# Where side work stands: sums of down weights moved by a few heads, and norm rows turned before they leave the chip

## The chip, the cores and the metric

The kernel runs on one core of one Trainium2 chip. The metric is the device time of one execution in microseconds (us). The core has TensorE (PE, with its weight loads as PEld), VectorE (DVE), ScalarE (ACT), GpSimd (POOL) and SyncE (SP), which here issues most DMAs; each engine works off its own queue in order, and waits on semaphores.

## What is computed

One layer of a diffusion backbone over 2048 latent tokens of width 1024, with 256 context tokens. Cut to what matters here:

```python
h   = modulate(rms_norm(x, g1), shift_a, scale_a)     # adaLN: modulation from c
q, k, v, g, f = split(h @ w_in)                        # 4 retention heads of 128, a Fourier part of 512
r   = retention(q, k, v)  (two scans, chunks of 128, states started from the context) * silu(g)
z   = real(fft2(f over positions and channels))        # 4 groups
m   = concat(r, z) @ w_out                             # output projection
x   = x + gate_a * rms_norm(m, g2)
h   = modulate(rms_norm(x, g3), shift_b, scale_b)
y   = conv3 over each image row of (h @ w_up); y = gate * value
x   = x + gate_b * rms_norm(y @ w_down, g4)
```

The inputs are fp32. The output has the shape of x.

## The kernel before

**Arithmetic.** A product of two fp32 matrices is made of three passes: each operand is split into a rounded part and the rest (`split`: ACT casts `hi`, VectorE subtracts to get `lo`), and `mm3` (lines 90, 91, 92) multiplies hi·hi, hi·lo and lo·hi into one PSUM tile. Tokens lie in the free dimension in four blocks `b` of 512, channels in the partitions in eight tiles of 128.

**Stages, in order of time.** Modulation, context and the weights of its keys `wk` (to 80 us); four blocks of v products with their norm, `adaw` being the modulation weights for the second half of the layer (80 to 186); heads 0 to 3, about 100 us each, as generators of strips (`k_strip`, `q_strip`: products of one block) and cores (`k_core`, `q_core`: states and chunk products), walked by one loop over `units`; the Fourier stage (to about 750); the output projection, 32 steps of `mix_mm(b, n)` (block b, output tile n), into `psmix` tiles that ACT seeds with the Fourier half (`seed_mix`, two steps ahead); then two passes of up products and two of down products.

**Who sets the order.** The code is written in one order, and a scheduler reorders it on each engine: an instruction whose inputs and buffers are there may move ahead of others. `tc.keep_in_program_order(i)` ties an instruction to its written place. Within the output projection a table `steps` says after which of the 32 steps a thing is written (`at(t, f, ...)`).

**Down sums.** The up and down products of later stages use sums of weight blocks. `w_sums()` makes those of the down weights in 22 chunks: two loads of 256 KB (line 205), four VectorE operations of 128×256 (line 220), one store of 512 KB to `wd` (line 222). Its buffer pool holds two chunks. It is written in the Fourier stage (`some_sums`, one `next` per operation).

**Norm rows.** A norm over channels needs sums over partitions: `sum_cols` multiplies squares with ones into `pc` (line 160), VectorE scales (`rp`, line 128), POOL raises to the power −0.5 (line 129) and leaves a column tile of 128×4 (`rcm` for the projection, `r2c` for the second norm, `rcf` at the end). To multiply along tokens it must become a row on all partitions: for the first blocks by TensorE and ACT (`bcast_row`: `pb`, `rr_`), for others through DRAM: `row_out` writes the column (line 133), `row_in` reads it back to all partitions (line 138).

**Hand-over.** In the last steps of the output projection the first up products start (`psu`); their weights come by `ur<-in_w_up` (line 1152), are split to `u_a`, and are taken by `operands`. `mt` and `m` (lines 964, 967), `h`, `b`, `t` (1037, 1040, 1041) are what is made of the projection's result: residual, norm, modulation and the sums of blocks. `late_h` makes `xn` of a block that is needed only later.

## Time and profile before

| | us |
|---|---|
| median of 3 runs | 2201.43 |
| the 3 runs | 2195.55, 2201.43, 2203.13 |
| the profiled execution | 2195.93 |
| its span in the trace | 2194.2 |
| PE busy in the span | 2076.4 (95%) |
| DVE busy | 1615.2 (74%) |
| ACT busy | 1009.2 (46%) |
| POOL busy | 616.7 (28%) |

The span is that of the instructions on the core; 1.7 us of the execution lie around it. Busy time is counted over the whole span, and the stages differ. The granted clock of TensorE is written as a share of its full speed, 2.4 GHz; where it is 0.5 the other level, 1.2 GHz, was granted.

### The profile page before, as it was taken

The numbers are of one execution on the slowest core, as the hardware profiler recorded it, in microseconds if no ns is written. First come the engines' busy times: TensorE is split into PE (matmuls) and PEld (weight loads), VectorE is DVE, ScalarE is ACT, GpSimd is POOL, SyncE is SP. The second block draws the span as 40 slices with busy tenths as digits, with TensorE's granted clock in tenths as the row PEclk, the third lists the DMA queues.
The fourth block names the chain that finished last, engine by engine and source line by source line (L and its number), as shares of the span: only waits on it lengthen the run. The fifth ranks groups of instructions, "written<-read, shape, count | busy, mean of one in ns | idle before, by whom it ended". The sixth has DMA issues, their size and how long they took to land.

```text
span 2194.2 us, 28116 instructions
## 1 busy us (share of the span) xinstructions
PE 2076.4 (95%) x9819; PEld 1711.4 (78%) x9819; DVE 1615.2 (74%) x2346; ACT 1009.2 (46%) x1754; POOL 616.7 (28%) x496
## 2 busy tenths in 40 slices
PE   7899899999899977989989999999999999999996
PEld 3777778888798866778778888887887888878886
DVE  6876877767566387998898886778777777775557
ACT  4342233324444566544545554545555455553441
POOL 4101122323101243242343342021333334331025
PEclk9999999999999988999999999999999999999998
DMA  8676643232562155664564478665355655386653
GB/s 306 213 242 216 192 139 92 100 96 95 146 223 100 52 199 139 183 207 176 183 205 159 154 275 297 218 242 177 135 187 197 185 185 178 135 272 224 200 154 130
DMA packets 202590, 395.20 MB, mean 180 GB/s; under 512 B 31816, under 2 KB 69584, under 8 KB 202448
## 3 DMA queue, kind: packets, MB, share of 16 engines
q1 hardware_dynamic: 194416, 367.07, 51.6%
q0 software_dynamic: 7600, 26.23, 3.3%
q8 instruction: 77, 1.26, 0.2%
q14 instruction: 65, 0.53, 0.1%
q10 hardware_dynamic: 432, 0.11, 0.0%
HBM read 275.33 MB, written 118.00 MB: 179 GB/s over the span
## 4 chain that ended last, share of the span: by engine, by line
PE 56%; DVE 22%; DMA 10%; issue 6%; ACT 3%; POOL 2%; SPq 1%; DVEq 0%; ACTq 0%; POOLq 0%
PE psu L90 8%; PE psu L91 8%; PE psu L92 8%; PE psd L90 5%; PE psd L91 5%; PE psd L92 5%; DMA ur<-in_w_up 2%; DVE u_a L83 2%; DVE y L1259 1%; DVE u_s L83 1%; DVE fd L638 1%; DMA wsum<-in_w_down 1%; DMA adaw<-in_wadaB 1%; PE pada L86 1%; DMA wd<-wsum 1%
## 5 line engine op out<-in xcount | busy, mean ns | idle before, releaser
L83 DVE TENSOR_TENSOR dlo<-draw,dhi 128x1024 fp32r<-128x1024 f32 x154 | 200.3, 1323 | 113.7 <-ACT dhi L82 102.4
L91 PE MATMUL psd<-dlo,dhi 128*128 128x512 f32 (+1 forms) x660 | 247.1, 375 | 2.9 <-DVE dlo L83 2.9
L92 PE MATMUL psd<-dhi,dlo 128*128 128x512 f32 (+1 forms) x660 | 246.2, 375 | 0.0
L1297 POOL TENSOR_TENSOR y<-y,y 128x512 f32<-128x512 f32 x82 | 127.0, 1549 | 388.5 <-DVE y L1260 274.5
L82 ACT CAST dhi<-draw 128x1024 fp32r<-128x1024 f32 x154 | 159.7, 1051 | 162.2 <-PE psd L92 116.5
L90 PE MATMUL psd<-dhi 128*128 128x512 f32 (+1 forms) x660 | 209.4, 375 | 0.6 <-DVE cx L1558 0.6
L91 PE MATMUL psu<-t,u_s 128*128 128x512 f32 x492 | 194.1, 395 | 1.4 <-DVE t L83 1.4
L90 PE MATMUL psu<-t,u_s 128*128 128x512 f32 x492 | 194.9, 396 | 0.0
L92 PE MATMUL psu<-t,u_s 128*128 128x512 f32 x492 | 193.9, 394 | 0.0
L83 DVE TENSOR_TENSOR u_a<-ur,u_a 128x512 fp32r<-128x512 f32 x147 | 139.7, 953 | 61.3 <-ACT u_a L82 60.8
L90 PE MATMUL psu<-b,u_a 128*128 128x512 f32 x424 | 165.6, 391 | 3.1 <-ACT u_a L82 1.9
L91 PE MATMUL psu<-b,u_a 128*128 128x512 f32 x424 | 165.2, 390 | 0.0
L92 PE MATMUL psu<-b,u_a 128*128 128x512 f32 x424 | 165.2, 390 | 0.0
L91 PEld LDWEIGHTS psd<-dlo,dhi 128*128 128x128 f32 x660 | 124.2, 188 | 25.6 <-DVE dlo L83 3.3
L92 PEld LDWEIGHTS psd<-dhi,dlo 128*128 128x128 f32 x660 | 124.2, 188 | 22.3
L90 PEld LDWEIGHTS psd<-dhi 128*128 128x128 f32 x660 | 123.3, 188 | 23.2 <-DVE cx L1558 0.8
L82 ACT CAST u_a<-ur 128x512 fp32r<-128x512 f32 x147 | 90.6, 620 | 103.0 <-PE psu L92 92.3
L1256 ACT ACTIVATE y<-psu,cb,cw 128x512 f32<-128x512 f32 x135 | 104.2, 775 | 19.0 <-DVE psu L1405 13.7
L83 DVE TENSOR_TENSOR u_s<-us,u_s 128x512 fp32r<-128x512 f32 x103 | 84.7, 823 | 38.4 <-ACT u_s L82 38.3
L91 PEld LDWEIGHTS psu<-t,u_s 128*128 128x128 f32 x492 | 94.1, 191 | 22.0 <-DVE t L83 1.9
L90 PEld LDWEIGHTS psu<-t,u_s 128*128 128x128 f32 x492 | 94.1, 191 | 19.9 <-ACT psu L1394 0.9
L92 PEld LDWEIGHTS psu<-t,u_s 128*128 128x128 f32 x492 | 93.8, 191 | 20.0
(438 smaller groups left out, 5313.9 us busy)
## 6 DMA issues: line engine op xcount, KB each, us to landing
ur<-in_w_up SPq DMA_DIRECT2D x74, 512.0 KB, 5.5
draw<-wd SPq DMA_DIRECT2D x88, 256.0 KB, 5.6
draw<-ft SPq DMA_DIRECT2D x88, 256.0 KB, 5.8
ft<-y SPq DMA_DIRECT2D x36, 512.0 KB, 5.5
draw<-in_w_down SPq DMA_DIRECT2D x66, 256.0 KB, 5.1
draw<-fb SPq DMA_DIRECT2D x66, 256.0 KB, 5.3
xt<-in_xT SPq DMA_DIRECT2D x56, 256.0 KB, 4.0
adaw<-in_wadaB SPq DMA_DIRECT2D x24, 512.0 KB, 6.5
```

The lines of the kernel that those rows point to most:

```text
L82: nc.scalar.copy(hi, src)
L83: nc.vector.tensor_tensor(lo, src, hi.bitcast(F32), op=ALU.subtract)
L86: nc.tensor.matmul(ps, l, r, start=start, stop=stop)
L90: nc.tensor.matmul(ps, lhi, rhi, start=start, stop=False, skip_group_check=on)
L91: nc.tensor.matmul(ps, lhi, rlo, start=False, stop=False, skip_group_check=on)
L92: nc.tensor.matmul(ps, llo, rhi, start=False, stop=stop, skip_group_check=on)
L638: tc.keep_in_program_order(nc.vector.tensor_tensor(o_, a_, b_, op=op))
L1256: nc.scalar.activation(y, ps, AF.Identity, bias=cb[:, j:j + 1], scale=cw[:, j, 1:2])
L1259: nc.vector.scalar_tensor_tensor(y3[:, :, 1:64], p3[:, :, 0:63], cw[:, j, 0:1], y3[:, :, 1:64], ALU.mult, ALU.add)
L1297: nc.gpsimd.tensor_tensor(y1, y1, y2, op=ALU.mult)
```

## The change

Five edits. (1) All eight `wk` tiles are cast by ACT; POOL and VectorE only subtract. (2) The down sums are written in heads 1 to 3, one step after every fourth piece, and in smaller doses in the Fourier stage; the first load of each chunk is tied to its place. (3) `row_out` turns the column by a TensorE product with the identity into PSUM (`prow`, 4×128), VectorE copies it (`rowt`), and the DMA writes four runs of 128 numbers. `row_in` is tied to its place. (4) The writing of rows is taken out of `mix_cols` and `x2_cols` into functions of its own, called a step later. (5) In the output projection, the loads of `rt`, the first norms, the first load of up weights and the first four splits stand at other steps, and those four casts are tied.

```diff
-        def split(hi, lo, src):
-            nc.scalar.copy(hi, src)
+        def split(hi, lo, src, tie=False):
+            c = nc.scalar.copy(hi, src)
+            if tie:
+                tc.keep_in_program_order(c)
             nc.vector.tensor_tensor(lo, src, hi.bitcast(F32), op=ALU.subtract)
...
         def row_out(rc, n, name, eng=None):
             d = dp.tile([n * P], F32, tag="row_" + name, name="row_" + name)
-            (eng or nc.sync).dma_start(d.rearrange("(i p) -> p i", p=P), rc)
+            pr = pmt([n, P], "prow")
+            mm(pr, rc, ident, True, True)
+            t = cp.tile([n, P], F32, tag="rowt", name="rowt")
+            nc.vector.tensor_copy(t, pr)
+            (eng or nc.sync).dma_start(d.rearrange("(i p) -> i p", p=P), t)
             return d
...
         def row_in(rt, d, n, name, eng=None):
             rr = rt([P, n * P], "rr_" + name)
-            (eng or nc.sync).dma_start(rr, bass.AP(tensor=d.tensor, offset=d.offset, ap=[[0, P], [1, n * P]]))
+            r = (eng or nc.sync).dma_start(rr, bass.AP(tensor=d.tensor, offset=d.offset, ap=[[0, P], [1, n * P]]))
+            tc.keep_in_program_order(r)
...
-                        nc.sync.dma_start(w[:, 2 * i:2 * i + 2], A["w_down"][k + KH * i].rearrange("p (n c) -> p n c", n=2)[:, :, c])
+                        ld = nc.sync.dma_start(w[:, 2 * i:2 * i + 2], A["w_down"][k + KH * i].rearrange("p (n c) -> p n c", n=2)[:, :, c])
+                        if i == 0:
+                            tc.keep_in_program_order(ld)
...
-            if kt % 2:
-                nc.scalar.copy(w[:, 0], src)
-                nc.gpsimd.tensor_tensor(w[:, 1], src, w[:, 0].bitcast(F32), op=ALU.subtract)
-            else:
-                nc.vector.tensor_copy(w[:, 0], src)
-                nc.vector.tensor_tensor(w[:, 1], src, w[:, 0].bitcast(F32), op=ALU.subtract)
+            nc.scalar.copy(w[:, 0], src)
+            (nc.gpsimd if kt % 2 else nc.vector).tensor_tensor(w[:, 1], src, w[:, 0].bitcast(F32), op=ALU.subtract)
...
                 npiece += 1
                 if npiece % (KSTEP if sf is k_strip else QSTEP) == 0:
                     next(folds, None)
+                if o.h and npiece % 4 == 2:
+                    some_sums(1)
...
                 p1 = zprod(2 * part, lt)
-                some_sums(2)
+                some_sums(1)
...
         def mix_cols(b):
             rcm[b] = cst([P, 4], f"rcm{b}", po_)
             sum_cols(accm[b], rcm[b], 4, po_)
-            if b > 1:
-                rowm[b] = row_out(rcm[b], 4, f"m{b}")
+
+        def mix_out(b):
+            rowm[b] = row_out(rcm[b], 4, f"m{b}")
...
         def x2_cols(b):
             sum_cols(accx[b], r2c[:, 4 * b:4 * b + 4], 4, po_)
-            if b:
-                r2d[b] = row_out(r2c[:, 4 * b:4 * b + 4], 4, f"n{b}")
+
+        def x2_out(b):
+            r2d[b] = row_out(r2c[:, 4 * b:4 * b + 4], 4, f"n{b}")
...
-                split(w[:, 0], w[:, 1], a[nme])
+                split(w[:, 0], w[:, 1], a[nme], not bb and len(early) < 4)
...
-                at(RS[0] * b + RS[1] * k // 2, load_r, b + 1, k)
+                at(KT * b + 1 + k, load_r, b + 1, k)
...
-            at(t + 6, x2_cols, b)
-            at(t + 7, x2_rows, b)
+            at(t + 7, x2_cols, b)
+            at(t + 8, x2_rows, b)
+        at(26, x2_out, 1)
         at(27, mix_cols, 2)
+        at(28, mix_out, 2)
...
-        at(26, lambda: up0.append(up_load(0)))
+        at(25, lambda: up0.append(up_load(0)))
         early = []
-        for n in range(4):
-            at(28, lambda: early.append(next(up0[0][2])))
...
+            if t in (28, 29):
+                early.extend(next(up0[0][2]) for _ in range(2))
...
         def rest_of_mix():
             mix_cols(3)
+            yield
+            mix_out(3)
+            yield
...
                 x2_cols(b)
+                yield
+                x2_out(b)
                 yield
```

Here RS was (8, 4) and KT is 8: the loads of the next block stood at steps 0, 2, 4 and 6 of a block, and stand at 1, 2, 3 and 4.

Where instructions come to stand, at three places. First VectorE at the beginning of head 1, before: the rotation of keys (`kT`), a difference of the Fourier part (`fd`), a scaled key (`kzb`) and the states `S`.

```order
L638 TENSOR_TENSOR fd_3_2462<-h_0_779 128x512
L561 TENSOR_SCALAR kzb<-ptk,EXT 128x512
L500 TENSOR_TENSOR kT_0_2350<-psk,rpt 128x512
L501 TENSOR_TENSOR kT_0_2350<-kT_0_2350,rpt 128x512
L502 TENSOR_TENSOR kT_0_2350<-kT_0_2350,sw 128x512
L575 SCALAR_TENSOR_TENSOR S_0_2467<-S_0_2467,EXT,pkv 128x128 x3
L575 SCALAR_TENSOR_TENSOR S_1_2471<-S_0_2467,EXT,pkv 128x128
```

The same place after:

```order
L643 TENSOR_TENSOR fd_3_2470<-h_0_779 128x512
L229 TENSOR_TENSOR wsum<-wsum 128x256 x3
L566 TENSOR_SCALAR kzb<-ptk,EXT 128x512
L229 TENSOR_TENSOR wsum<-wsum 128x256
L505 TENSOR_TENSOR kT_0_2350<-psk,rpt 128x512
L229 TENSOR_TENSOR wsum<-wsum 128x256
L506 TENSOR_TENSOR kT_0_2350<-kT_0_2350,rpt 128x512
L229 TENSOR_TENSOR wsum<-wsum 128x256
L507 TENSOR_TENSOR kT_0_2350<-kT_0_2350,sw 128x512
L580 SCALAR_TENSOR_TENSOR S_0_2476<-S_0_2476,EXT,pkv 128x128
```

Six sums stand between those operations. Before, the 88 stood in VectorE's order from the WK matrices to the end of head 0; now 13 stand at the end of head 0, 55 in head 1 and 20 in the key strips of head 2, none elsewhere.

Second, ACT at the end of the output projection, before: `m` leaves `psmix`, `psmix<-m` is a seed, `sq` a square for a norm, `u_a` the first splits of up weights.

```order
L1007 COPY m_3_5902<-psmix 128x512
L154 ACTIVATE sq<-psmix 128x512
L82 CAST u_a_7299<-ur_7219 128x512
L82 CAST u_a_7302<-ur_7219 128x512
L82 CAST u_a_7305<-ur_7220 128x512
L82 CAST u_a_7308<-ur_7220 128x512
L1041 ACTIVATE h_7311<-h_7311,modB 128x512
L82 CAST t_0_7318<-m_0_5899 128x512
L996 COPY psmix<-m_3_6094 128x512
L1007 COPY m_3_5966<-psmix 128x512
L1007 COPY m_3_6030<-psmix 128x512
```

The same place after:

```order
L1015 COPY m_3_5975<-psmix 128x512
L161 ACTIVATE sq<-psmix 128x512
L81 CAST t_0_7310<-m_0_5972 128x512
L1004 COPY psmix<-m_3_6149 128x512
L1015 COPY m_3_6032<-psmix 128x512
L1051 ACTIVATE h_7303<-h_7303,modB 128x512
L1015 COPY m_3_6092<-psmix 128x512
L1051 ACTIVATE h_7304<-h_7304,modB 128x512
L81 CAST b_1_7315<-h_7304 128x512
L81 CAST u_a_7322<-ur_7198 128x512
L81 CAST u_a_7325<-ur_7198 128x512
```

The last seed (`psmix<-m`) stood behind four `u_a` casts, and stands ahead of the first.

Third, SP's queue at that time, before: `row_n` and `row_m` are the rows, `x` stores of the projection's result, `xt` loads of the input.

```order
L133 DMA row_n_7144<-r2c 128x4x1
L1152 DMA ur_7219<-in_w_up 128x1024
L1009 DMA x_2_3_119<-m_3_6030 128x512
L1152 DMA ur_7220<-in_w_up 128x1024
L133 DMA row_m_7263<-rcm_7254 128x4x1
L1009 DMA x_3_3_123<-m_3_6094 128x512
L957 DMA xt_7798<-in_xT 128x512
L138 DMA rr_n_10637<-row_n_7144 128x512
L1152 DMA ur_7295<-in_w_up 128x1024
```

The same place after:

```order
L1162 DMA ur_7198<-in_w_up 128x1024
L1162 DMA ur_7199<-in_w_up 128x1024
L1017 DMA x_2_3_119<-m_3_6092 128x512
L139 DMA row_n_7221<-rowt 4x128
L1017 DMA x_3_3_123<-m_3_6149 128x512
L1017 DMA x_4_3_127<-m_3_5975 128x512
L139 DMA row_m_7297<-rowt 4x128
L1017 DMA x_5_3_131<-m_3_6032 128x512
```

The first two `ur` loads stand ahead of `row_n`, and both rows leave from `rowt`, a tile of 4×128.

## Rows read from the trace of the kernel before

**Rows 1.** Busy time of each engine by stretch of the span, core 0, with the mean granted TensorE clock (1.00 is full) and the DMA engines' busy share behind it: WK and context (39 to 80), v products (80 to 186), heads 0 to 3, output projection with the hand-over, the stage behind it, and the first down pass. Columns: stretch in us: its length, busy time (instructions) of PE, PEld, DVE, ACT, POOL, then PEclk, DMA share, GB/s.
```profile
39.00:80.00 41.00, 33.08 (x144) 26.25 (x145) 31.85 (x57) 18.68 (x39) 11.20 (x9) 0.86 0.48 160
80.00:186.00 106.00, 100.44 (x440) 81.20 (x440) 83.39 (x147) 45.23 (x74) 4.19 (x3) 0.95 0.73 233
186.00:292.00 106.00, 93.97 (x487) 78.28 (x485) 82.51 (x169) 28.61 (x79) 23.78 (x21) 0.95 0.65 206
292.00:387.00 95.00, 92.32 (x521) 78.64 (x520) 68.85 (x127) 31.20 (x89) 25.82 (x23) 1.00 0.35 99
387.00:486.00 99.00, 94.00 (x527) 79.78 (x526) 71.93 (x129) 31.36 (x89) 26.16 (x23) 1.00 0.32 95
486.00:586.00 100.00, 95.66 (x526) 80.83 (x524) 64.48 (x97) 42.64 (x94) 27.59 (x22) 0.98 0.43 121
...
752.00:861.00 109.00, 86.97 (x377) 70.04 (x376) 75.13 (x99) 69.06 (x128) 42.36 (x26) 0.87 0.57 158
861.00:1000.00 139.00, 130.30 (x558) 105.39 (x557) 130.31 (x179) 74.36 (x125) 50.83 (x29) 0.98 0.59 192
...
1300.00:1500.00 200.00, 200.00 (x884) 165.62 (x883) 145.14 (x152) 99.39 (x115) 46.52 (x52) 1.00 0.69 239
```

**Rows 2.** The tile `wsum` (the down sums): operation, count, duration in ns as min/median/max, first and last start in us; and, from the waits of SP's queue within 186 to 292 us, what SP stood on before a load of it (us in total, times, longest).
```profile
L220 DVE TENSOR_TENSOR wsum<-wsum x88: 408/418/1441, 62.6 to 297.4; 128x256 f32<-128x256 f32 x88
L205 SPq DMA_DIRECT2D wsum<-in_w_down x44: 539/600/1520, 36.3 to 281.3; - x44
...
SPq L205 <- DMA wd<-wsum: 25.2, 9, 5.9
```

**Rows 3.** TensorE's timeline at 55 to 60 us (start, length, engine, line and operation, and in brackets the idle time before it with what ended it), and the tile `wk`: two of its operations, and one line of who waited for it.
```profile
56.10 0.73 PE L90 MATMUL psc<-wk,hc 128*128 128x512 f32 x2 [3.00 <-DVE wk L414]
59.18 0.80 PE L91 MATMUL psc<-wk,hc 128*128 128x512 f32 x1 [2.35 <-DVE wk L415]
...
L411 ACT CAST wk<-wkr x4: 618/620/622, 53.6 to 55.2; 128x512 fp32r<-128x512 f32 x4
L412 POOL TENSOR_TENSOR wk<-wkr,wk x4: 1437/1450/1720, 54.3 to 58.5; 128x512 fp32r<-128x512 f32 x4
...
  ACT kz L424: 11.7, 1
```

**Rows 4.** v products: TensorE's timeline at two of its sums of squares, and VectorE's group of `wsum` within 80 to 186 us (busy us, mean ns, idle time before it and what ended that).
```profile
123.97 1.02 PE L160 MATMUL pc<-ones,acc 128*128 128x1 f32 x8 [1.92 <-DVE acc L155]
...
152.03 0.69 PE L160 MATMUL pc<-ones,acc 128*128 128x1 f32 x5 [2.31 <-DVE acc L155]
...
L220 DVE TENSOR_TENSOR wsum<-wsum 128x256 f32<-128x256 f32 x31 | 12.3, 419 | 6.9 <-DMA wsum<-in_w_down 6.7
```

**Rows 5.** Head 0 (186 to 292 us): one stall in TensorE's timeline, VectorE's group of `wsum`, and a small load's median landing time (issues, KB each, us); last, from SP's waits in head 1 (292 to 387), what the loads of v stood on.
```profile
266.28 0.66 PE L627 MATMUL pto<-ident,sT 128*128 128x128 f32 x2 [3.24 <-DVE sT L623]
...
L220 DVE TENSOR_TENSOR wsum<-wsum 128x256 f32<-128x256 f32 x45 | 20.5, 457 | 12.4 <-DMA wsum<-in_w_down 11.0 <-issue 0.8
...
S<-sini SPq DMA_DIRECT2D x2, 64.0 KB, 3.4
...
SPq L506 <- PE pkv L86: 15.5, 4, 6.9
```

**Rows 6.** Output projection: the stalls in TensorE's timeline, and two pieces of the chain of waits (start, length, what) at the sum of squares that `row_n` carries.
```profile
781.87 1.41 PE L160 MATMUL pc<-ones,accx 128*128 128x1 f32 x6 [4.06 <-DVE accx L155]
...
813.00 0.73 PE L90 MATMUL psmix<-rt,wr 128*128 128x512 f32 x2 [3.18 <-ACT rt L82]
816.45 0.80 PE L91 MATMUL psmix<-rt,wr 128*128 128x512 f32 x1 [2.72 <-DVE rt L83]
...
851.17 0.80 PE L90 MATMUL psmix<-rt,wr 128*128 128x512 f32 x1 [8.80 <-ACT psmix L996]
...
824.30 0.80 PE pc L160 x8
825.44 1.03 POOL r2c L129
```

**Rows 7.** The hand-over: ACT's timeline; the traffic of 826 to 852 us in 40 slices of 0.65 us; two DMA issues within it (count, KB each, median us to landing), and the first of them over the whole span; last, the window behind the hand-over with the columns of rows 1.
```profile
848.36 1.14 ACT L82 CAST u_a<-ur 128x512 fp32r<-128x512 f32 x2 [6.75 <-DMA ur<-in_w_up]
...
850.53 0.58 ACT L996 COPY psmix<-m 128x512 f32<-128x512 f32 x1
...
GB/s 0 0 3 0 0 13 13 25 69 25 38 44 38 25 25 13 25 19 63 309 236 391 373 376 320 167 63 16 60 35 22 38 69 91 227 221 224 293 356 384
...
ur<-in_w_up SPq DMA_DIRECT2D x4, 512.0 KB, 14.1
...
row_n<-r2c SPq DMA_DIRECT2D x1, 2.0 KB, 11.4
...
ur<-in_w_up SPq DMA_DIRECT2D x74, 512.0 KB, 5.5
...
852.00:866.00 14.00, 14.00 (x54) 11.34 (x54) 12.93 (x18) 10.62 (x20) 4.82 (x3) 0.85 0.67 252
```

**Rows 8.** First up pass: two stalls in TensorE's timeline; and, from the tile `row_n`, who waited for it (us, times).
```profile
942.93 0.50 PE L90 MATMUL psu<-t,u_a 128*128 128x512 f32 x1 [2.43 <-DVE psf L1408]
...
1153.21 0.79 PE L90 MATMUL psu<-t,u_a 128*128 128x512 f32 x1 [5.21 <-DVE psf L1408]
...
  POOL rr_n L138: 19.0, 2
```

15 lines of the change are left out of this document (7 added, 8 removed).

## Prediction

> **What bounds the kernel now.** I read the windows by stage first [rows 1]. TensorE is busy in nearly all of every stage, so what matters is where it isn't. A stage without loss exists: from 1300 to 1500 it is busy 200.00 of 200 us at granted clock 1.00. For the others I take as loss the idle time plus (1 − clock) times the stretch, since a stretch at half clock does half its work. That gives 7.9 + 5.7 = 13.7 us in 39–80 (the WK matrices), 5.6 + 5.3 = 10.9 in 80–186 (v products), 12.0 + 5.3 = 17.3 in head 0 (186–292), only 2.7, 5.0 and 6.3 in heads 1, 2 and 3, then 22.0 + 14.2 = 36.2 in the output projection with its hand-over to the up products (752–861), and 8.7 + 2.8 = 11.5 in 861–1000. What is worth having lies in five places, and all five are touched by the diff.
>
> Next I asked what these stages hold that the quiet ones don't. The tile view of the sums [rows 2] shows 88 VectorE operations of 418 ns in the median and 44 loads, started from 36 to 297 us: although the code asks for them in the Fourier stage, 31 of them run in 80–186 (12.3 us) [rows 4] and 45 in head 0 (20.5 us) [rows 5]. The queue view shows SP standing 25.2 us in head 0 on `wd<-wsum`, a store's landing, before it may issue the next load [rows 2]; vb, fscr and strip loads stand in line behind that. The idle times of TensorE [rows 3 to 6] then name what comes last: VectorE nearly everywhere up to head 0, and at 851.17 a wait of 8.80 us for the ACT copy that seeds `psmix`, more than any other of these rows.
>
> **The change part by part.**
>
> *WK casts.* TensorE waits 3.00 and 2.35 us for a VectorE cast and subtraction of `wk` at 56–59 us, and the clock dip around it is in the 5.7 us of clock loss of that stretch [rows 1, 3]. VectorE casts four pages and subtracts four; after, ACT casts all eight at 0.62 us, 5.0 us in a row from about 53.6, and VectorE only subtracts. The first page is then ready near 54.2, and its product no longer waits until 56.10. The extra 2.5 us on ACT are covered: ACT waits 11.7 us behind its four casts [rows 3]. But POOL's four subtractions of 1.45 us end about where they did (54.8 + 5.8 = 60.6, before 58.5 + 1.7), so the last pages gain nothing. I take −4; bounds −1 (only the first page matters) and −8 (both waits and half the dip).
>
> *v products without sums.* 31 sums and some eight chunks of loads and stores leave. VectorE loses 12.3 us of work and a 6.7 us wait for a sum's load that blocked everything behind it [rows 4]. The stalls there that name VectorE sum to 1.92 + 2.31 = 4.2 us, each followed by a clock dip. Of the 10.9 us I take −5; bounds 0 (the dips come anyway) and −9.
>
> *Head 0 without sums.* 45 sums leave. Heads 1 to 3, nearly without sums, lose (2.7 + 5.0 + 6.3)/3 = 4.7 us, head 0 17.3. The difference, 12.6 us, is 0.28 us of TensorE time per sum. The stall of 3.24 us [rows 5] is on sT, a VectorE result in a queue full of sums. Some of head 0's loss may belong to its beginning (strips and modB arriving), so −10; bounds −5 and −13.
>
> *Heads 1 and 2 with sums.* The order of VectorE after the change puts 13 sums at the end of head 0, 55 in head 1 and 20 at the start of head 2, and none later, so they do not come to the Fourier stage in either kernel. Head 1 has 95 − 68.85 = 26 us of idle VectorE and takes 55 × 0.43 = 24 us of work. So it will be fuller than head 0 was (82.5 of 106 us is 78%, 93 of 95 is 98%). Two things differ from head 0: the `adaw` work is over, and the code asks for one sum every four pieces. Bounds: 0 (all of it falls into idle time) and 75 × 0.28 = +21 (head 0's rate). I take +12, a little nearer to the dear end, since head 0 is the nearest case of this kind, and its rate holds the cost of stores landing late as well.
> The Trainium skill ("GPSIMD Engine Reference", sections Specifications and Key points) says that GpSimd shares its SBUF interfaces with VectorE and contends with VectorE instructions that have two SBUF inputs, which the sums have. The trace leans that way only a little: a sum averages 457 ns in head 0, where POOL is busy 23.78 us, against 419 (a row's mean) in 80–186, where it is busy 4.19, while the longest took 1441 [rows 1, 2, 4, 5]. By the row's means the surcharge on 75 sums is 3 us of VectorE time; what the rule could do at most is the fourth rival below.
>
> *Output projection, order of seeds and casts.* Before, ACT has four `u_a` casts in its queue ahead of the last seed copy. They wait for `ur`, the second pair 6.75 us, so the seed runs at 850.53 and TensorE's `psmix` product at 851.17 [rows 6, 7]. `ur` is late while `row_n` and `row_m` fly, 512 elements of 4 bytes each: in the first 7 us from 826 the traffic falls to some 0 to 70 GB/s, `row_n` takes 11.4 us to land for 2 KB, and the four `ur` beside them 14.1 in the median instead of 5.5 [rows 7]. After, the last seed copy stands ahead of the first `u_a` cast, `ur` is issued ahead of the rows, and the rows leave as 4 descriptors of 512 B. So the 8.80 us go. The last load of rt for a block moves two steps earlier (step 4 of 8 instead of 6), which should take away 3.18 + 2.72 us. The 4.06 us on accx at 781.87 stay: the order before that sum is unchanged. Half-clock stretches after those stalls hold up to 14.2 us. Against it: removing 14.7 us (8.80 + 3.18 + 2.72) of idle TensorE time lets it run into VectorE, which from 852 to 866 is already busy 12.93 of 14 us and in 861–1000 130.31 of 139 [rows 1, 7, 8]. TensorE cannot bank what VectorE cannot feed. I take −12 of the 14.7 us of idle time and the clock that follows; bounds −5 and −20.
>
> *861 to 1200.* Stalls of 2.43 and 5.21 us on `psf` [rows 8] come from a full VectorE. The reorder puts the late `xn` (rows of image block 1) later by about 100 rows, so the 5.21 may go, and the rows' DMAs no longer hold POOL for 19.0 us in sum [rows 8]. Hardly any VectorE work leaves, though. I take −4; bounds 0 and −9.
>
> *Turned rows.* Each of eight rows adds a product, a PSUM-to-SBUF copy of 4×128 on VectorE, and a wait of TensorE for the POOL power that makes the column. No row shows that product; the nearest are eight `pc` products in 0.80 us and the wait behind such a group, so each costs from 0.1 to about 1.5 us; the first stands behind a broadcast that waits for the same column in both kernels, for six of them 12 or more other products stand between column and turn in the new order, for the last only two. Between a `pc` group and its POOL power lay 1.4 us (824.30 + 0.80 to 825.44 + 1.03, [rows 6]), which two products don't cover: a wait of about 1 us at the end. I put +2 on this, and −2 on the later rows landing faster (11.4 us for `row_n` before [rows 7], 3.4 for a load of 64 KB in head 0 [rows 5]): 0; bounds −2 and +3.
>
> Sum: −4 − 5 − 10 + 12 − 12 − 4 + 0 = −23. Against the profiled execution, 2195.93, that is 2173. The three runs have the median 2201.43, 5.5 above it; I expect the median after to lie somewhat above its fast end too, and say 2175.
>
> **The rivals.**
> 1. *VectorE bounds the hand-over.* The seed stall goes but TensorE then waits for VectorE at 855–900: the fifth term (hand-over) becomes −4 and the sixth 0. For it: the 12.93 of 14 us [rows 7]. Against: the stall also idled VectorE for 8 us, work that it now does earlier. Sum −11 instead of −23, so 2187 (12 above the forecast; the others are counted in the same way).
> 2. *The heads hide the sums.* The fourth term is 0: 2163. For it: 26 us of idle time in head 1 and the spread placement. Against: head 0's 0.28 us per sum.
> 3. *Slower: SP's queue moves its stall into head 1.* Loads wait for stores to land (25.2 us in head 0), with vb and strip loads behind, and head 1's S chain stands on vb. It decides when the fourth term exceeds +12 + 23 + 7 = +42, 0.48 us for each of 88 sums, more than a whole sum's 0.42 and 1.7 times head 0's rate. For it: 95 us hold 55 sums where head 0 held 45 in 106. Time at 0.55 each: 2175 + 48 − 12 = 2211. Against: in head 1 SP already stood 15.5 us until TensorE freed a vb buffer [rows 5], so these loads are early and have room.
> 4. *Sums collide with POOL.* POOL is busy 25.82 of 95 us in head 1. If each sum under it took the longest row, 1.44 instead of 0.42, that is 0.27 × 75 × 1.0 = 20 us more of VectorE; at 0.6 of it on the path (0.28 of 0.457) +12, so 2187. This is what the rule of the Trainium skill named above would do at most; the trace's mean of 457 ns speaks against it.
>
> **How the numbers follow.** A difference under 0.3% (6.6 us) cannot be told from none here. Forecast 0.47 (2165 to 2185), rival 1 0.18, rival 2 0.16, rival 4 0.11, rival 3 0.08. All cases but the third end under 2194.8, but the forecast's and the first and fourth rival's own spread (each bound is some 8 us) puts about 0.09 into the band from 2194.8 to 2208. So faster 0.84, same 0.10, slower 0.06. Range 2156 to 2199: from rival 2 with the hand-over at −19, to rivals 1 and 4 together (2175 + 12 + 12 = 2199).
>
> **What would show it.** Sums: no `wsum` in 36–270, and losses of about 5 us in head 0 and 12 to 20 in head 1. The WK waits at 56–59 gone. In the hand-over no wait of `psmix` for ACT, `ur` landing in 5 to 7 us, rows in 2 to 4. Wrong would be: SP standing on `wd<-wsum` for over 25 us in head 1; a `psu` wait for VectorE of over 5 us behind the last `psmix`; a `prow` product waiting over 2 us; or head 0's loss staying at 17, which would say that the sums were not its cause.

## The result and the profile after

The changed kernel takes 2181.35 us in the median of 4 runs (2179.43 to 2182.94); the kernel before, on the same chip, 2199.54 (2195.55 to 2203.13). The ratio is 0.992 with a 95% interval of 0.9905 to 0.9934: 18.2 us faster by the medians, clear of the 0.3% that can't be told from nothing. The forecast was 2175, range 2156 to 2199. Its profiled execution took 2182.37 us with a span of 2180.6, against 2195.93 and 2194.2: 13.6 us between the two profiles, since the profiled run before lies at the low end of its runs and the one after near the high end of its own. Of the 23 us that the forecast gave between profiles 59% came; of the 24.5 from the median before, as measured on this chip, down to its 2175, 74%.

I cut both traces at the same instructions: the first v product, the first key strip product of each head, the first `psmix` product, and the 374th up product (a tenth of all up products; the first up pass ends with half of them). Lengths in us, each boundary the start of that product in TensorE's timeline:

| stage | before | after | difference | forecast |
|---|---|---|---|---|
| start to v (WK) | 80.1 | 75.9 | −4.2 | −4 |
| v products | 104.7 | 98.5 | −6.2 | −5 |
| head 0 | 106.7 | 97.5 | −9.2 | −10 |
| heads 1 and 2 | 194.8 | 213.4 | +18.6 | +12 |
| head 3 and Fourier stage | 242.1 | 242.8 | +0.7 | 0 |
| projection and hand-over | 220.5 | 209.0 | −11.5 | −12 |
| rest of the first up pass | 361.7 | 361.8 | +0.1 | −4 |
| second up and both down passes | 883.6 | 881.7 | −1.9 | 0 |

When the projection begins, at 728.0 after against 728.3 before, nothing of the gain of 19.6 us in the first three rows is left. All that the change brings in the end comes out of the projection and what follows. How good a single profile is shows where runs of the table further below share a stage's code: head 0 with the sums at their old place took 106.5 to 106.8 us, but the v products 100.7 to 104.7, and head 3 with the Fourier stage, where no sums stand, 242.1 to 246.6. In those two stages a difference of 4 us is not sure.

The windows after, with the columns of [rows 1]: WK, v, heads 0 to 2, projection with hand-over, and the stage behind it.

```profile
39.00:76.00 37.00, 33.46 (x146) 26.06 (x147) 26.39 (x44) 20.76 (x42) 11.82 (x9) 0.88 0.29 102
76.00:174.00 98.00, 96.06 (x432) 77.17 (x432) 73.26 (x116) 45.18 (x74) 4.92 (x3) 0.98 0.58 182
174.00:272.00 98.00, 91.89 (x492) 77.03 (x491) 70.34 (x135) 29.16 (x79) 24.88 (x21) 0.98 0.41 124
272.00:385.00 113.00, 96.52 (x527) 80.39 (x525) 92.23 (x180) 31.50 (x90) 25.15 (x23) 0.98 0.67 208
385.00:485.00 100.00, 94.64 (x523) 80.77 (x522) 77.38 (x149) 31.33 (x89) 24.89 (x23) 0.98 0.49 147
752.00:843.00 91.00, 80.95 (x357) 65.41 (x356) 64.70 (x89) 61.77 (x115) 39.71 (x24) 0.91 0.47 160
843.00:1000.00 157.00, 147.97 (x634) 119.20 (x633) 148.24 (x203) 86.69 (x148) 58.40 (x32) 0.98 0.56 191
```

By the measure of the forecast (idle time plus clock) the v products lose 1.9 + 2.0 = 3.9 us instead of 10.9, head 0 8.1 instead of 17.3, head 1 16.5 + 2.3 = 18.7 instead of 2.7, and the projection's stretch 10.1 + 8.2 = 18.2 instead of 36.2. VectorE is busy 92.23 of 113 us in head 1, where it was busy 68.85 of 95 [rows 1].

TensorE's timeline of the changed kernel in WK (columns of [rows 3]):

```profile
54.49 0.73 PE L91 MATMUL psc<-wk,hc 128*128 128x512 f32 x2 [1.19 <-ACT wk L419]
```

The same in head 1:

```profile
275.05 0.50 PE L93 MATMUL psk<-h,sp_k 128*128 128x512 f32 x1 [2.59 <-DVE sp_k L84]
...
289.67 0.63 PE L632 MATMUL pto<-ident,sT 128*128 128x128 f32 x4 [3.71 <-DVE sT L628]
...
302.74 0.63 PE L562 MATMUL ptk<-ident,kT 128*128 128x128 f32 x4 [1.61 <-DVE kT L507]
```

VectorE's group of sums within head 1 (columns of [rows 5]):

```profile
L229 DVE TENSOR_TENSOR wsum<-wsum 128x256 f32<-128x256 f32 x55 | 25.2, 468 | 8.8 <-DMA wsum<-in_w_down 6.3 <-issue 2.2
```

What SP stood on there (us in total, times, longest):

```profile
SPq L212 <- DMA wd<-wsum: 25.0, 12, 4.5
```

Two places of VectorE's timeline there, ahead of TensorE's wait at 289.67:

```profile
281.30 1.34 DVE L229 TENSOR_TENSOR wsum<-wsum 128x256 f32<-128x256 f32 x3 [3.23 <-DMA wsum<-in_w_down]
...
287.98 1.54 DVE L628 TENSOR_TENSOR sT<-oc,rc 128x512 f32<-128x512 f32 x1 [1.12 <-POOL rc L130]
```

The first `wk` product starts at 54.49 after 1.19 us of waiting for ACT, where it stood 3.00 us until 56.10 [rows 3]. In head 1 the waits look as those of head 0 did [rows 5]: strips, sT and kT, all VectorE's. The 55 sums take 468 ns in the mean, and SP stands 25.0 us on the landing of stores, as it stood 25.2 in head 0 before [rows 2]. The scene has moved, almost number for number. VectorE itself stands 6.3 us in head 1, and stood 11.0 in head 0 before [rows 5], at a sum whose load has not landed; everything behind that sum in its queue stands too, and the longest of TensorE's waits, 3.71 us for sT, comes 8 us behind such a stand of 3.23 us. Read so, the loads and stores of the sums reach TensorE through VectorE's queue too, and not through SP's alone; no run takes this way apart from the others.

The hand-over of the changed kernel in TensorE's timeline:

```profile
820.99 1.87 PE L167 MATMUL pc<-ones,accx 128*128 128x1 f32 x8 [3.92 <-DVE accx L162]
```

And at the last `psmix` product:

```profile
842.38 0.39 PE L93 MATMUL psmix<-rt,wr 128*128 128x512 f32 x1
842.60 0.47 PE L91 MATMUL psu<-b,u_a 128*128 128x512 f32 x1
```

ACT's timeline at the last seed:

```profile
837.05 0.59 ACT L1004 COPY psmix<-m 128x512 f32<-128x512 f32 x1
...
841.90 1.14 ACT L81 CAST u_a<-ur 128x512 fp32r<-128x512 f32 x2
```

The traffic of 822 to 852 us in 40 slices of 0.75 us, and the issues of `ur` in it (count, KB each, median us to landing):

```profile
GB/s 194 235 412 432 426 360 186 5 38 314 14 8 0 319 30 0 0 0 0 3 347 3 115 235 0 11 339 60 328 388 426 186 202 240 240 360 333 432 415 426
...
ur<-in_w_up SPq DMA_DIRECT2D x6, 512.0 KB, 5.8
```

From the view of the tile `row_f`, the landing of its DMAs as far as the trace has it, which is for the last row, written from `rowt` and read back (of the other seven writes it has none):

```profile
DMA to landing us min/median/max: 2.4/3.2/4.0
```

The last seed is at 837.05, ahead of the `u_a` casts at 841.90; the last `psmix` product at 842.38 is followed by the first up product at 842.60. The wait of 8.80 us [rows 6] is gone, the traffic lies low for 4.5 us at most, where it did so for over 7 [rows 7], and `ur` lands in 5.8 us instead of 14.1. New is a wait of 3.92 us on accx at 820.99 (an earlier one is longer, 5.09 where it was 4.06): the loads of rt came in time, the 3.18 and 2.72 us of [rows 6] went, and TensorE ran into the next thing that VectorE had not finished. At 831 us it stood where it had stood before (the 337th of 384 `psmix` products starts at 831.1 us, before at 831.3); the last one starts 13.6 us earlier.

### The profile page after: what moved, and what is told of

Its sections match the earlier page's. It is cut to its first block, busy times and chain, and to the rows that moved or that the text cites. A ratio compares the mean times of both kernels' runs of the same rounds, so it can differ in the third digit from the quotient of the medians.

```text
span 2180.6 us, 28151 instructions
## 1 busy us (share of the span) xinstructions
PE 2075.9 (95%) x9835; PEld 1706.1 (78%) x9835; DVE 1613.2 (74%) x2350; ACT 1011.4 (46%) x1758; POOL 627.1 (29%) x496
## 5 line engine op out<-in xcount | busy, mean ns | idle before, releaser
L81 ACT CAST u_a<-ur 128x512 fp32r<-128x512 f32 x147 | 90.5, 620 | 97.8 <-PE psu L93 97.8
```

The source lines that it names most:

```text
L81: c = nc.scalar.copy(hi, src)
```

## The experiments

Theories. For the heads: **D**, a sum costs TensorE time because VectorE makes it between two results that TensorE waits for; **Q**, because SP stands on the landing of a chunk's store before the next load, with other loads behind. For the projection: **M**, the writes of 4 bytes make all transfers late; **N**, the place of the last seed behind the casts is what costs.

One table for all runs. Sums by stage, stage lengths as above, and the median with the ratio's interval against the kernel before on the same chip:

| run | sums in v / head 0 / 1 / 2 / 3 / Fourier | v | head 0 | head 1 | head 2 | head 3 and Fourier | projection, hand-over | median us | ratio (95%) |
|---|---|---|---|---|---|---|---|---|---|
| before | 31 / 45 / 3 / 0 / 0 / 0 | 104.7 | 106.7 | 96.2 | 98.6 | 242.1 | 220.5 | 2199.54 | |
| after | 0 / 14 / 55 / 19 / 0 / 0 | 98.5 | 97.5 | 112.8 | 100.6 | 242.8 | 209.0 | 2181.35 | 0.9905 to 0.9934 |
| before_turned_rows | 31 / 45 / 3 / 0 / 0 / 0 | 100.7 | 106.8 | 97.9 | 97.8 | 246.6 | 214.2 | 2191.69 | 0.9949 to 0.9982 |
| rows_not_turned | 0 / 14 / 55 / 19 / 0 / 0 | 99.3 | 99.6 | 110.2 | 101.3 | 243.2 | 214.3 | 2198.42 | 0.9983 to 1.0016 |
| sums_old_place | 31 / 45 / 3 / 0 / 0 / 0 | 104.1 | 106.5 | 98.0 | 98.4 | 244.6 | 208.3 | 2183.42 | 0.9906 to 0.9952 |
| sums_in_fourier | 0 / 0 / 0 / 0 / 0 / 80 | 98.3 | 94.2 | 97.1 | 97.9 | 278.0 | 208.5 | 2195.06 | 0.9969 to 0.9996 |
| sums_spread | 0 / 0 / 27 / 29 / 32 / 0 | 98.4 | 94.9 | 100.4 | 107.6 | 250.1 | 208.2 | 2180.92 | 0.9885 to 0.9938 |
| load_late_heads | 0 / 7 / 17 / 20 / 19 / 25 | 98.9 | 95.2 | 102.3 | 100.5 | 260.8 | 208.6 | 2186.99 | 0.9899 to 0.9937 |
| load_late_fourier | 0 / 0 / 0 / 0 / 0 / 68 | 98.1 | 94.2 | 97.0 | 98.0 | 277.6 | 208.3 | 2198.59 | 0.9968 to 0.9995 |
| heads_gpsimd_queue | 0 / 0 / 54 / 34 / 0 / 0 | 99.7 | 94.3 | 120.4 | 110.9 | 244.4 | 208.5 | 2197.90 | 0.9975 to 1.0004 |
| fourier_gpsimd_queue | 0 / 0 / 0 / 0 / 5 / 74 | 99.1 | 95.1 | 96.5 | 98.3 | 295.0 | 208.5 | 2211.68 | 1.003 to 1.007 |
| sums_on_gpsimd | 0 / 0 / 88 in heads 1 to 3 | 97.9 | 93.9 | 103.2 | 114.5 | 263.1 | 208.3 | 2206.32 | 1.0019 to 1.0044 |
| sums_left_out | none | 98.4 | 94.8 | 112.8 | 101.1 | 248.4 | 209.0 | 2189.43, one run | |
| sums_without_traffic | 0 / 0 / 26 / 29 / 33 / 0 | 102.5 | 105.0 | 101.7 | 104.3 | 248.3 | 209.1 | 2191.33, one run | |

Where a row doesn't add up to 88, the rest lies ahead of the v products or in the projection. The three runs with sums in the Fourier stage give the heads without any sum: 94.2 to 95.1, 96.5 to 97.1, and 97.9 to 98.3 us.

### The rows and the order

**before_turned_rows.** Of the change only the new `row_out`.

```diff
-            (eng or nc.sync).dma_start(d.rearrange("(i p) -> p i", p=P), rc)
+            pr = pmt([n, P], "prow")
+            mm(pr, rc, ident, True, True)
+            t = cp.tile([n, P], F32, tag="rowt", name="rowt")
+            nc.vector.tensor_copy(t, pr)
+            (eng or nc.sync).dma_start(d.rearrange("(i p) -> i p", p=P), t)
```

> The kernel before with one part of the change alone: the rows turned by TensorE and written as four runs of 128 numbers; order of seeds, loads and casts as before. Theory M (the writes of 4 bytes make the up weights late, and with them the last seed): ur lands in 5 to 7 us, the wait of 8.80 us for the seed shrinks under 3, the first up products begin 6 to 9 us earlier, and the time is 6 to 9 us under the kernel before. Rival N (the place of the seed behind the casts is the cause, the rows only fly beside it): at least 6 of the 8.80 us stay, the time is within 3 us of the kernel before.

2191.69 us, 6.8 under the 2198.51 of the kernel before beside it. Its ACT timeline at the last seed:

```profile
840.02 2.18 ACT L82 CAST u_a<-ur 128x512 fp32r<-128x512 f32 x4
...
842.62 0.60 ACT L1000 COPY psmix<-m 128x512 f32<-128x512 f32 x1
```

Its issues of `ur` from 822 to 852 us:

```profile
ur<-in_w_up SPq DMA_DIRECT2D x7, 512.0 KB, 4.5
```

One turned product in its TensorE timeline:

```profile
834.70 0.38 PE L86 MATMUL prow<-ident,rcm 128*4 128x128 f32 x2 [0.78 <-POOL rcm L129]
```

The four casts still stand ahead of the seed, and cost nothing: `ur` lands in 4.5 us, they run through from 840.02, and the seed follows at 842.62 instead of 850.53 [rows 7]. Theory M. A turned product waited 0.78 us for the power. One sign of M did not come: the first up product starts no earlier than before (842.84 us against 841.14); what comes earlier is the last `psmix` product, at 845.9 instead of 856.0.

**rows_not_turned.** The reverse of that edit, in the changed kernel.

> The changed kernel with one part undone: the rows leave as 512 elements of 4 bytes again, the new order of seeds, loads and casts stays. Theory M (the writes make the up weights late): the last seed no longer waits, but the first up products stand for the casts behind a late ur; 4 to 9 us slower than the changed kernel, 2185 to 2190. Rival N (the order is what counts): within 2 us of it, 2179 to 2184.

2198.42 us, ratio 0.9983 to 1.0016: all that the change had gained is gone, more than theory M asked for. Its traffic and its issues of `ur` from 822 to 852 us:

```profile
GB/s 322 68 0 3 0 0 11 33 60 27 44 33 33 16 33 22 22 71 377 399 380 329 299 49 63 22 11 38 63 107 93 131 101 142 265 391 382 377 374 412
...
ur<-in_w_up SPq DMA_DIRECT2D x8, 512.0 KB, 10.4
```

VectorE's timeline 400 us later:

```profile
1245.05 0.75 DVE L1046 SCALAR_TENSOR_TENSOR xn<-xn,a,rr_n 128x512 f32<-128x512 f32 x1 [8.04 <-DMA rr_n<-row_n]
```

TensorE's timeline there:

```profile
1249.63 0.79 PE L91 MATMUL psu<-t,u_a 128*128 128x512 f32 x1 [7.28 <-DVE psf L1421]
```

Two issues from 1232 to 1252 us:

```profile
rr_n<-row_n SPq DMA_DIRECT2D x1, 256.0 KB, 9.4
...
row_n<-r2c SPq DMA_DIRECT2D x1, 2.0 KB, 11.0
```

`ur` again takes 10.4 us, and the hand-over is 5.3 us longer than in the changed kernel. The other part comes at 1232: the new order puts the late `xn` beside the next row's write. That write takes 11.0 us, the `rr_n` beside it 9.4, `xn` waits 8.04 us for it, and TensorE 7.28 behind VectorE. In the changed kernel the same two waits are there, but shorter:

```profile
1235.19 0.75 DVE L1050 SCALAR_TENSOR_TENSOR xn<-xn,a,rr_n 128x512 f32<-128x512 f32 x1 [3.60 <-DMA rr_n<-row_n]
...
1239.95 0.50 PE L91 MATMUL psu<-t,u_a 128*128 128x512 f32 x1 [2.42 <-DVE psf L1425]
```

There `rr_n` is issued at 1230.18, ahead of the next row's write at 1236.80, and lands in 5.0 us; how much of that is the turned row and how much the place in the queue, no run separates. So the two edits are a pair. In the projection they add up: turned rows alone −6.3, the new order alone (with the moved sums and the WK casts) −6.2, all edits −11.5 us. But the order alone gives its 6.2 back: the rest of the first up pass takes 369.2 us instead of 361.7. Turned rows alone give 4.7 back in their one profile (366.4), though their median stays 6.8 below; together they give nothing back (361.8).

### Where the sums stand

**sums_old_place.** The sums as before, all else as after.

```diff
-                        if i == 0:
-                            tc.keep_in_program_order(ld)
...
-                if o.h and npiece % 4 == 2:
-                    some_sums(1)
...
-                some_sums(1)
+                some_sums(2)
```

> The changed kernel with one part undone: the down sums are written in the Fourier stage again and no load of them is tied, so that they run in the v products and head 0 as before. Theory A (a sum costs TensorE about 0.2 us in every head, and moving them from head 0 to heads 1 and 2 only moves the loss): the stages up to head 2 lose again what they gained and head 1 gains it back, so that the output projection begins within 3 us of the changed kernel's 728 us, and the time is 2179 to 2184. Rival B (the sums' move is worth the 3 us of the forecast or more, and something else in the heads took it back): the projection begins at 731 us or later, and the time is 2185 or more.

2183.42 us, the projection at 728.8 us. Theory A of this run: the intervals of the two kernels overlap, and the move of the sums is worth nothing that can be measured. Against the heads without sums, the old place costs 6 us in the v products, 12 in head 0 and about 1 in head 1; the new one 3 in head 0, 16 in head 1 and 3 in head 2.

**sums_in_fourier.** The same, with the tie kept.

> The changed kernel with the sums written in the Fourier stage in the old doses, but with the first load of each chunk tied as in the change, so that all 88 run from about 600 to 755 us. Theory A (what a sum costs is how full VectorE is where it stands; in 586 to 752 us it is busy about 96 of 166 us while TensorE hardly waits): the heads keep the gain of 17 us that the trace shows at the end of head 0, the Fourier stage takes the 37 us of sums in its idle time, the projection begins at 710 to 714 us, and the time is 2163 to 2168. Rival B (a sum costs 0.2 us wherever it stands, by the chain of loads and stores on one queue): the projection begins at 726 to 732 us, the time is 2180 or more. Rival C (the products of the Fourier stage and the loads of rt stand behind the sums): waits of over 3 us for rt or m, and over 2185.

The heads behaved as theory A said: at the end of head 2 this kernel is 22.7 us ahead of the changed one. Then it lost 35 in the Fourier stage and ended at 2195.06. TensorE's timeline there:

```profile
659.04 0.73 PE L91 MATMUL psab<-tab,z 128*128 128x512 f32 x2 [2.02 <-ACT tab L81]
...
672.54 0.37 PE L91 MATMUL psp<-a,wpm 128*128 128x2 f32 x1 [3.70 <-ACT wpm L81]
...
678.24 0.37 PE L91 MATMUL psp<-a,wpm 128*128 128x2 f32 x1 [3.99 <-ACT wpm L81]
```

What SP stood on from 596 to 740 us:

```profile
SPq L212 <- DMA wd<-wsum: 33.4, 13, 4.0
```

TensorE waits for tables (`tab`) and for weights that GpSimd makes from loads (`wpm`); these loads stand on SP behind the sums', and SP stands 33.4 us on stores. The tables landed in 5.3 us in the median, in the changed kernel in 8.8, so they were late by their issue and not by the transfer. None of the three theories had these waits: A was right for the heads alone, B gave a smaller loss, and C named rt and m. VectorE was idle 18 of 60 us between 640 and 700 us. That an engine has idle time in a stage did not mean that work could be put there: the stage also lived on loads that came in time.

**fourier_gpsimd_queue, heads_gpsimd_queue.** `nc.sync.dma_start` for the sums' loads and stores becomes `nc.gpsimd.dma_start`, in sums_in_fourier and in the changed kernel.

> The sums in the Fourier stage (as in sums_in_fourier), but with their loads and stores issued by GpSimd, whose queue has little else there. Theory Q (the tables came late because SP stood 33 us on the landing of stores): the waits for tab and wpm go, the projection begins at 706 to 716 us, the time is 2160 to 2171. Rival B (the tables came late because the DMA engines were 85% busy, or because VectorE splits wpm and tab behind the sums): most of the 35 us that the Fourier stage lost stays, the projection begins at 730 us or later, the time is 2185 or more.

> The changed kernel with the loads and stores of the sums issued by GpSimd instead of SP. Theory Q (SP's queue is the cost in heads 1 and 2): at least 8 of the 19 us come back, 2168 to 2174. Theory D (VectorE is): within 3 us of the changed kernel, or slower where GpSimd's part of the rotation waits behind a store's landing: 2179 to 2190.

Both are slower than their models: 2211.68 and 2197.90 us, the second slower than either theory allowed. In the first the projection begins at 758.2 us, late as rival B had it; one of its long waits from 596 to 758 us is VectorE's before sums whose loads had not landed:

```profile
DVE wsum L229 <- DMA wsum<-in_w_down: 31.1, 6, 8.5
```

The waits of GpSimd in heads 1 and 2 of the second:

```profile
POOL wd L231 <- DVE wsum L229: 35.9, 11, 5.7
...
POOL wsum L212 <- DMA wd<-wsum: 27.9, 10, 5.6
```

It stands 35.9 us until VectorE has made the sums that it is to store, and 27.9 on stores, and the second half of the rotation stands behind that in its queue. This says nothing for D or Q; it says that here a wait on the landing of a store was no cheaper on GpSimd's queue.

**load_late_heads, load_late_fourier.** The next load is written ahead of the last sum of a chunk.

```diff
-                nxt = begin() if todo else None
                 yield
...
+                    if q == 3 and todo:
+                        nxt = begin()
```

> The changed kernel with one thing moved: the next chunk's load is written just ahead of the last of the four sums of a chunk, not ahead of the first, so that the store before it has had three steps of time to land when SP comes to the load. The sums spread to the output projection by this. Theory Q (SP standing on stores is the cost): SP stands under 8 us on wd in all (31.8 in the changed kernel), heads 1 and 2 take 96 to 102 us each, the projection begins at 712 to 720 us, 2166 to 2174 us. Theory D: the same cost per sum at other places, the projection begins at 726 to 730 us, 2179 to 2184.

> The sums in the Fourier stage (as in sums_in_fourier) with the next chunk's load written just ahead of the last of the four sums. Theory Q: SP's 33 us of standing on wd in the Fourier stage fall under 12, tab and wpm come in time, the projection begins at 706 to 716 us, 2160 to 2171 us. Theory B (the DMA engines or VectorE are full there): at least half of the 35 us that this stage lost stays, 2180 or more.

2186.99 and 2198.59 us. In the Fourier stage SP's standing on `wd` went from 33.4 only to 28.8 us, and before stores it now stood 27.1 us until VectorE was done. SP's waits of load_late_fourier from 596 to 742 us:

```profile
SPq L212 <- DMA wd<-wsum: 28.8, 12, 4.0
SPq L233 <- DVE wsum L231: 27.1, 7, 13.4
```

TensorE's timeline there:

```profile
674.58 0.37 PE L91 MATMUL psp<-a,wpm 128*128 128x2 f32 x1 [7.32 <-ACT wpm L81]
```

TensorE still waits for `wpm`, 7.32 us at once. Theory Q asked for under 12 us of standing and got 28.8, so it wasn't tested there. In load_late_heads SP stood on `wd` for 2.9 us in all from 174 to 740 us, and heads 1 and 2 took 102.3 and 100.5 us for 37 sums: 5.3 and 2.6 us more than without. That is 7.9/37 = 0.21 us for a sum, where the changed kernel paid (15.7 + 2.7)/74 = 0.25: most of the price stayed with SP's standing gone, and theory Q falls as the whole of it. But the traffic's part had not gone with it: VectorE stood 5.9 us in these heads at sums whose loads, issued late, had not landed.

```profile
L231 DVE TENSOR_TENSOR wsum<-wsum 128x256 f32<-128x256 f32 x37 | 18.2, 498 | 6.3 <-DMA wsum<-in_w_down 5.9
```

And 25 sums that now slid into the Fourier stage cost about 14 us there (260.8 − 242.8, less 4 for the 19 sums in head 3), so that the projection began at 732.6 us and the time lies above what either theory gave.

**sums_left_out.** The VectorE operations go, loads and stores stay.

> The changed kernel without the 88 VectorE operations of the down sums (their loads and stores stay, so the weights that go to wd are not summed and the output is not the reference's). Theory D (VectorE's time is what the sums cost the heads): heads 1 and 2 get back 14 to 18 of the 19 us that they lost against the kernel before, the projection begins at 710 to 714 us. Theory Q (SP's queue, which stands on the landing of each store with the loads of v and of strips behind it, is the cost): they get back under 6 us, the projection begins at 722 us or later.

Head 1 took 112.8 us, as with its 55 sums. Its window of head 1 (columns of [rows 1]):

```profile
269.00:382.00 113.00, 98.11 (x526) 82.31 (x524) 69.17 (x123) 31.59 (x90) 25.57 (x23) 0.97 0.78 242
```

SP's waits in it:

```profile
SPq L232 <- DMA wsum<-in_w_down: 28.4, 16, 4.1
SPq L212 <- DMA wd<-wsum: 9.4, 7, 3.2
```

These are the numbers that theory Q asked for: VectorE is back at 69.17 us, and TensorE is idle for 14.9 us where it was for 16.5 with the sums. But the run did not take one thing away: without sums a store waits on SP for its load to land, 28.4 us in all, and 50 of the 66 transfers' issues crowded into head 1. It shows that the traffic, so crowded, can cost 16 us by itself. It doesn't show what it costs in the changed kernel.

**sums_without_traffic.** The sums at spread places on two buffers loaded once; all loads and stores early.

> As sums_spread, with the 88 VectorE operations at the same places in heads 1 to 3, but on two buffers that are loaded once: all loads and stores of chunks are issued early, in the v products and head 0, and move the weights unsummed (so the output is not the reference's). Heads 1, 2 and 3 hold VectorE's part of the sums alone. Theory D (VectorE's time is the cost): heads 1 and 2 take 100 and 107 us as in sums_spread, and the stretch from head 3 to the projection 250. Theory Q (the traffic on SP's queue is): 96 to 98 us each, and 242 to 244 for that stretch, as without sums.

Its heads 1 and 2 as windows (columns of [rows 1]):

```profile
284.00:386.00 102.00, 96.28 (x526) 82.09 (x526) 78.36 (x151) 31.39 (x89) 25.86 (x23) 0.97 0.30 88
386.00:490.00 104.00, 96.49 (x524) 81.62 (x523) 82.15 (x156) 31.27 (x89) 26.07 (x23) 0.97 0.31 89
```

VectorE's group of sums in both:

```profile
L234 DVE TENSOR_TENSOR wsum<-wsum 128x256 f32<-128x256 f32 x55 | 26.9, 489 | 0.2
```

101.7 and 104.3 us: 4.6 and 6.4 more than without sums, 11.0 us for 55 sums, 0.20 us per sum, with 88 and 89 GB/s in flight where head 1 of the changed kernel had 208. VectorE alone is enough too, and it is busy 78 and 82 us of these heads, not 98%.

The same run holds the other half: 57 of its issues of loads and stores stand in the v products and head 0, where it makes no sums. Head 0 took 105.0 us, 10 to 11 more than the heads 0 without sums and nearly the 106.7 of before. Two of TensorE's waits in it, for a load and for a strip behind one:

```profile
205.07 0.50 PE L87 MATMUL pkv<-vb,kzf 128*128 128x128 f32 x2 [3.06 <-DMA vb<-vscr]
...
224.54 0.50 PE L91 MATMUL psg<-h,sp_g 128*128 128x512 f32 x1 [3.97 <-ACT sp_g L81]
```

So in a single run traffic alone costs head 0 about what sums with their traffic cost it before. The prices of the two parts do not add up to that of both.

**sums_spread.** Evenly over heads 1 to 3.

```diff
-                    nc.vector.tensor_tensor(w[:, o], w[:, l], w[:, r], op=op)
+                    d = nc.vector.tensor_tensor(w[:, o], w[:, l], w[:, r], op=op)
+                    if o == 3:
+                        tc.keep_in_program_order(d)
...
-                if o.h and npiece % 4 == 2:
+                if o.h and npiece % 8 in (2, 5, 7):
```

> The changed kernel with the first VectorE operation of each chunk of sums tied to its place too, and three steps of sums in every eight pieces instead of two, so that 28 or 29 sums stand in each of heads 1, 2 and 3 (55, 20 and none in the changed kernel). Theory D (VectorE is the cost, and a sum costs more the fuller VectorE is: 55 in head 1 cost 16.6 us, 20 in head 2 cost 2.1): 88 at about 0.1 us cost 9 us instead of 19, the projection begins at 716 to 720 us, the time is 2169 to 2174. Rival Q (each of 22 chunks costs its wait on SP's queue, wherever it stands): within 3 us of the changed kernel, 2179 to 2184.

2180.92 us, the same as the changed kernel, and the time that rival Q gave. Heads 1 and 2 cost 3.3 + 9.7 = 13.0 us for 56 sums (0.23 us each), and head 3 with the Fourier stage 7 more than in the changed kernel. So half the density did not make a sum cheaper, and theory D in the form that I had given it (the price rises with VectorE's fill) falls. Here VectorE did not stand before loads; its group of sums from 269 to 478 us:

```profile
L229 DVE TENSOR_TENSOR wsum<-wsum 128x256 f32<-128x256 f32 x59 | 29.6, 501 | 0.4
```

In sums_without_traffic these two heads lost 11.0 us, here 13.0: where the loads come in time, VectorE's part alone is enough for most of the price. That SP's standing, 21.8 us in these heads, adds little to it is likely and not shown.

**sums_on_gpsimd.** In sums_spread, `nc.vector.tensor_tensor` becomes `nc.gpsimd.tensor_tensor`.

> As sums_spread, with the 88 sums made by GpSimd instead of VectorE, at even places in heads 1 to 3; GpSimd is busy some 26 of 95 us there, and a sum of half the size of its 1.45 us subtraction would take it about 0.75 us, 22 us per head. Theory D (VectorE's own time is most of the cost, 15 of 19 us by sums_without_traffic): heads 1 and 2 take 97 to 100 us, the projection begins at 712 to 718 us, 2166 to 2173 us. Rival G (GpSimd's sums come in bursts of four ahead of the rotation's second half and of the norm's power, or slow VectorE by the SBUF interfaces that they share): the heads take 103 us or more each, 2181 or more.

2206.32 us, a little slower than the kernel before (0.19 to 0.44%). The sums in the view of their tile (ns as min/median/max):

```profile
L229 POOL TENSOR_TENSOR wsum<-wsum x88: 720/1054/1723, 276.3 to 603.6; 128x256 f32<-128x256 f32 x88
```

A step of the keys' rotation on VectorE within 269 to 500 us:

```profile
L508 DVE TENSOR_TENSOR kT<-kT,rpt 128x512 f32<-128x512 f32 x8 | 8.1, 1011 | 0.1
```

VectorE's wait for GpSimd's half of the rotation there:

```profile
DVE kT L509 <- POOL sw L506: 9.8, 6, 4.0
```

The same step in sums_spread, within 269 to 478 us:

```profile
L508 DVE TENSOR_TENSOR kT<-kT,rpt 128x512 f32<-128x512 f32 x8 | 7.0, 871 | 0.0
```

A sum takes 1.05 us there instead of 0.42, the rotation waits 9.8 us for GpSimd, and VectorE's own step went from 871 to 1011 ns. Rival G, by both of its ways as it looks; that the slower step comes from the shared interfaces no run shows by itself.

## Why the prediction was right, and where not

**WK, v products, head 0: right in place and size.** −4.2, −6.2 and −9.2 us against −4, −5 and −10; in the v products runs of the same code differ by 4 us, so that its size is sure to that alone. The runs with neither sums nor their traffic in head 0 (94.2 to 95.1 us) put the price of its 45 sums, traffic included, at about 12 us, the 12.6 that the heads' losses had given. The sign "no `wsum` in 36–270" was missed by a little: 12 sums start from 250.0 us on.

**Heads 1 and 2: the term that was mis-sized.** Forecast +12, measured +18.6 (16.6 in head 1, 2.0 in head 2); the dear bound was +21. These 6.6 us and the 4.1 of the up pass are more than the whole distance of 9.4 us between the forecast and the two profiles. The step that failed is the sentence that took a value between "all of it falls into idle time" and "head 0's rate". VectorE's idle time in a head did not take in a sum: with 17, 27, 29, 45 or 55 of them in a head, each cost 0.1 to 0.33 us, about 0.2 to 0.3 in most. With the rate that the trace of before gave, 0.28, the term is 21, and the sum of the first four terms is +2 instead of −7; measured it is −1.0. I had the number and paid for idle time that the price already counted. Heads 1 and 2 do not differ from head 0 in what the price comes from: a sum there stands ahead of the same kT, sT and kzb, and brings the same loads and stores.

**The hand-over: right in size, half right in its parts, and so in part by luck.** −11.5 against −12. The seed's 8.80 us went, and with the clock behind it that is all of the gain. The 5.9 us on rt went too, and came back as 3.92 on accx and a lost lead: the forecast had said that the 4.06 at 781.87 would stay (it did, at 5.09 us), and not that the next of its kind stood behind rt. Of the cause, the text named both the late `ur` and the order, and priced them together. Either alone takes away about 6 us, both 11.5.

**861 to 1200: the −4 came, and was lost behind it.** At a tenth of all up products the changed kernel leads by 11.6 us, at 40% of them (1209 us, before 1225) by 15.6; the 5.21 us at 1153 [rows 8] went, as forecast, while stalls of 2.4 to 2.5 us on `psf` stayed. By the half, the end of the pass, the lead is 11.4 again. The largest wait in that last part is the one at 1239.95 behind `xn`, 2.42 us: the new order moved the late `xn` to where it waits for `rr_n`, and the forecast had counted only what that move takes away. Of the first rival there is this much: VectorE is busy 148.24 of 157 us from 843 to 1000. No run tests these 4 us by themselves, and they are no more than what the rest of this pass differs by between before and before_turned_rows (361.7 and 366.4).

**Turned rows: right as far as shown.** The first rides behind the broadcast, the last waited 0.79 us where about 1 was forecast, and the last row's DMAs, the only ones with a landing in the trace for the write, now land in 2.4 and 4.0 us; the stage at the end is 3 us shorter. What the forecast had left out is that the new order needs the rows turned (rows_not_turned).

**The rivals.** That the heads hide the sums is refuted, by the trace and by sums_spread. That SP's queue carries the loss to head 1 and decides the time: SP did stand 25.0 us there, just the 25 that the forecast had named as a sign of being wrong, but the term stayed under the 42 at which that rival began; that SP's standing has a part in the loss is not refuted. That sums collide with GpSimd: a sum's mean in head 1 was 468 ns, 49 over the 419 of [rows 4], 2.7 us for 55; that is small. In sums_on_gpsimd a VectorE step with two inputs from SBUF took 1011 ns in the heads where GpSimd made the sums, and 871 in the same heads of sums_spread. That agrees with the Trainium skill ("GPSIMD Engine Reference", sections Specifications and Key points), by which GpSimd contends with such steps for its SBUF interfaces.

**What stays open.** Of the 16 us that head 1 lost in the changed kernel, how much is VectorE's and how much the traffic's: in single runs each alone was enough for most of such a loss (the traffic in head 1 of sums_left_out and in head 0 of sums_without_traffic, VectorE in heads 1 and 2 of the latter), and no run held the other exactly as it was. That the projection begins at 728 us with the sums at the old place and at the new fits a nearly constant price per sum; a place without that price was not found among heads, v products and Fourier stage. No version here beats the changed kernel.

## What to carry to other kernels

Side work that is moved keeps its price unless the new place differs in what the price came from; take the price per piece from the stage where it stands now, and don't set idle time against it a second time. Idle time of an engine in a stage says little about room there, if the stage also lives on loads behind the same queue. Side work with loads of its own has a second way to cost: an engine that works in order stands at the first piece whose load is late. The write of single elements was paid by its neighbours here: look for what else is in flight beside such a write, now and after every reordering.

## What the runs showed of the hardware

How far a write of 2 KB in 512 elements of 4 bytes reaches: it landed in 11.4 us in the kernel before and in 11.0 in rows_not_turned, and held up what flew beside it: loads of 512 KB landed in 14.1 and 10.4 us in the median, and a read of 256 KB in 9.4. With four runs of 512 bytes in its place the loads took 4.5 to 5.8, and the two DMAs of the last row 2.4 and 4.0. GpSimd's operation on 128×256 for a sum took 1.05 us in the median against VectorE's 0.42, and a step of VectorE in the same heads was 16% longer.
